# Two-layer hybrid trunk: in the MLP layers the low half of a split weight tile comes from a negated ScalarE copy and an accumulating DMA

## The chip, the cores and the metric

The kernel runs on one core of a Trainium2 chip. The number that counts is the device time in microseconds, the median of three runs: 1920.09 us (1918.94, 1920.09 and 1925.68). The profile is one further execution, whose own time is its span.

## What is computed

A trunk of two layers over 512 latent tokens and 256 context tokens, 1024 features wide. Each layer has a mixer (attention and spatial gating in layer 0, retention in layer 1) and then a gated MLP with a depthwise convolution of width 3 along the tokens. Around each sub-layer stand RMS norms, and a shift, scale and gate computed from a conditioning vector by the matrices `ada_w`. The change touches the MLP alone:

```python
D_MODEL, SEQ, CTX_LEN, DEPTH, D_FF, CONV_W = 1024, 512, 256, 2, 2816, 3

def conv_ffn(h, w_in, conv_w, conv_b, w_out):
    a = dwconv3(h @ w_in, conv_w, conv_b)
    gate, up = jnp.split(a, 2, axis=-1)
    return (jax.nn.silu(gate) * up) @ w_out

# in layer i, for the latent tokens; for the context tokens in layer 0 alone
    h = modulate(rmsnorm(x, norm_g[i, 2]), sh2, sc2)
    x = x + g2 * rmsnorm(conv_ffn(h, ffn_w_in[i], ffn_conv_w[i], ffn_conv_b[i], ffn_w_out[i]), norm_g[i, 3])
```

`w_in` is 1024 x 5632, `w_out` 2816 x 1024, all float32.

## The kernel before

**Split products.** Every large product is made in three passes on TensorE in a rounded 32-bit format (fp32r). An operand is held as two tiles: *hi*, the operand rounded to that format, and *lo*, the operand less hi. `mm3` (L86 to L90) computes hi times hi (L88), hi times lo (L89) and lo times hi (L90). So each pass of a weight needs both tiles. In the tile names the last letter is `r` for the raw tile, `h` for hi and `l` for lo.

**Units.** Weights come in units of 128 x 1024 float32, 524,288 bytes. `unit` (L67 to L72) takes a raw tile from a ring of three buffers (tag `raw`), loads it by a DMA that SyncE (SP) issues (`load`, L49 to L50), and calls `split` (L63 to L65): ScalarE (ACT) makes hi by a rounding copy (L64), VectorE (DVE) makes lo by a subtraction (L65). `slot` (L74 to L78) gives hi and lo their place: six pairs in turn in the MLP of layer 0, eight in that of layer 1 (`phase`, L80 to L84).

**The MLP.** `ffn` (from L1101) walks over 22 blocks j of 128 gate and 128 up features. For each block `project` takes two units, f`l`0`j` and f`l`1`j` (f012 is layer 0, the up half, block 2), and multiplies them with the normed input: `pc` is the product for the context tokens (hc, layer 0 only), `pf` that for the latent ones (hl). The first two blocks are done together (four units: f000, f010, f001, f011 in layer 0), with the latent tokens in two halves, since the input of the second half is still being made then. `gated` (L1148 to L1159) applies the convolution and the gate, and splits the result into g. Every second block, `w_out` takes two units fo`l``j` of the output matrix for two earlier blocks, and `out_pieces` (L376 to L395) adds their products (`wf`) into y on DVE (L391). So a layer has 44 f units and 22 fo units.

**Background jobs.** After every block, `bg(2)` moves on a background job by two steps. A job, `ada_half` (L193 to L255), computes half of a later shift, scale or gate: it clears an accumulator on POOL (L199), loads four raw tiles `ar` **from the same ring of three buffers**, and adds each into the accumulators on DVE: two operations per tile and token stream (L208). During the MLP of layer 0 there are six jobs with two streams (24 raw tiles, four DVE operations each), during that of layer 1 two jobs with one stream (8 raw tiles, two operations each).

**The start of an MLP** overlaps the end of the mixer before it. There `residual` (L298 to L319) and `build_h` (L331 to L355) make the MLP's input: ACT squares and sums (L274), POOL scales the sum (L279: wxb, wyb, wyd ...) and takes its power of -1/2 (L260: yb3r, xd3r ...), DVE and ACT apply it (L309, L318, L319: yr), TensorE transposes, ACT applies the shift and scale (L348: hb, hd) and rounds (L64: hl0b, hl0d).

**Order.** A scheduler puts the instructions of each engine into one fixed order when the program is built; each engine then works through its own order and waits on semaphores. This holds for SP and POOL too, where they issue DMAs. A load into a raw buffer waits until the last reader of that buffer's former content is done.

Of the kernel before, what the change touches and what calls it, by code (L numbers as in the profile page):

```python
# [36 lines left out]
class Trunk:  # L37
# [29 lines left out]
    def unit(self, src, name, dst=None):  # L67
        raw = self.bp.tile([P, 1024], F32, name=f"{name}r", tag="raw", bufs=3)
        self.load(raw, src)
        hi, lo = dst or self.slot(name)  # L70
        self.split(hi, lo, raw)
        return hi, lo  # L72
# [7 lines left out]
    def phase(self, ctx, name, extra):  # L80
        self.xp = ctx.enter_context(self.tc.tile_pool(name=name, bufs=1))
        self.extra = extra
        self.turn = 0
        return self.xp  # L84

# [42 lines left out]
    def ada_first(self, q, pool, native, tag):  # L128
        """shift and scale of a quarter of the features, latent and context, for the first sub-layer; a step per unit"""
        S, V, T = self.S, self.V, self.T  # L130
# [125 lines left out]

# [1 line left out]
    def rsq(self, w, name):  # L258
# [9 lines left out]
    def ssq(self, src, name, n):  # L268
        """mean square over the row, a half (n) at a time"""
        ss = self.sst.get(name)  # L270
        if ss is None:
            ss = self.sst[name] = self.bp.tile([P, 2], F32, name=f"ss{name}", tag="ss", bufs=8)
        junk = self.t2k(f"j{name}{n}", BF16)
        self.S.activation(junk, src, AF.Square, scale=1.0 / 32, accum_out=ss[:, n : n + 1])  # L274
# [23 lines left out]
    def residual(self, t, y, gate, src, last, name, xt):  # L298
        """y (final) -> x += rmsnorm(y) * gate; then x normed into y's place."""
        V = self.V  # L300
        self.load(xt, src)
        hv = [slice(0, 512), slice(512, 1024)]
        for n, h in enumerate(hv):
            self.ssq(y[:, h], f"y{name}{t}", n)
        for h in hv:
            V.tensor_tensor(out=y[:, h], in0=y[:, h], in1=gate[:, h], op=ALU.mult)
        r = self.rms(f"y{name}{t}")
        for n, h in enumerate(hv):
            V.scalar_tensor_tensor(out=xt[:, h], in0=y[:, h], scalar=r, in1=xt[:, h], op0=ALU.mult, op1=ALU.add)  # L309
            if last:  # L310
                self.load(self.out[t * P : (t + 1) * P, h], xt[:, h])
            else:
                self.ssq(xt[:, h], f"x{name}{t}", n)
        if last:
            return
        self.load(self.xd[t], xt)
        r = self.rms(f"x{name}{t}")
        V.tensor_scalar(out=y[:, hv[0]], in0=xt[:, hv[0]], scalar1=r, scalar2=None, op0=ALU.mult)  # L318
        self.S.activation(y[:, hv[1]], xt[:, hv[1]], AF.Copy, scale=r)  # L319
# [11 lines left out]
    def build_h(self, chunk, xn, ab, name):  # L331
        """chunk 2: context tokens, chunks 0 and 1: latent halves."""
        s = 1 if chunk == 2 else 0
# [23 lines left out]
    def hcols(self, t):  # L357
        """stationary views of token tile t: k -> (hi, lo)"""
        if t >= 4:
            c = slice((t - 4) * P, (t - 3) * P)  # L360
            return lambda k: (self.hc[0][:, k, c], self.hc[1][:, k, c])
        c = slice(t * P, (t + 1) * P)
        return lambda k: (self.hl[0][:, k, c], self.hl[1][:, k, c])

    def proj_t(self, ps, w, stream, half=None):
        """ps[feat, tokens] += w^T h, w a stationary unit"""
        h = self.hc if stream else self.hl
# [6 lines left out]

# [1 line left out]
    def out_pieces(self, feats, wo, y, toks, first, final, name, tag="B"):  # L376
        """y[t] (+)= sum over the group's feature tiles, one closure per half token tile;
        feats: list of (hi, lo)[feat, tokens]"""

# [21 lines left out]
    def out_last(self, A, B, y, toks, early, final, name):  # L401
        """the last two groups (feats, wo): group A of the early tokens, group B of these, both for the others"""
        e, o = toks[:early], toks[early:]
# [6 lines left out]
    def finisher(self, gates, src, ab, name, xts, last=False):  # L410
        """per finished token tile: the residual update, then the next sub-layer's input once a chunk is there"""
        done = {}
# [20 lines left out]

# [1 line left out]
    def sgu(self, y, xn):  # L435
# [178 lines left out]
    def project_pair(self, j, pr):  # L614
        """q, k, v of two heads, transposed; returns the steps"""
        w = [self.unit(self.a["hyb_qkv"][(4 * i + j) * P : (4 * i + j + 1) * P], f"w{'qkv'[i]}{j}") for i in range(3)]
# [56 lines left out]
    def bias_tiles(self, h, hd):  # L673
        """8 x (relative bias, or the mask) of the three kinds of query tile"""
        G, ap = self.G, self.ap
# [13 lines left out]
    def score(self, h, b, pr, hd):  # L689
        """softmax of one query tile (b = 4: both context tiles), queries on partitions"""  # L690
        S, V, T, ap = self.S, self.V, self.T, self.ap
# [63 lines left out]
    def weigh(self, h, b, pr, hd):  # L755
        """keys onto partitions, and after a head's last tile the weighted values"""
        S, V, T = self.S, self.V, self.T
# [35 lines left out]

# [1 line left out]
    def retention(self, y, final):  # L795
        S, V, T, G, a = self.S, self.V, self.T, self.G, self.a
        KS = float(np.float32(P) ** np.float32(-0.5))
        with ExitStack() as ctx:
# [19 lines left out]
            def decay(h):  # L818
                """powers of the two decays: within a chunk, of the keys, of the queries, of a chunk"""
                d = hd[h]  # L820
# [35 lines left out]
            def k_nat(h):  # L856
                """keys onto partitions, decayed towards the end and towards the start of their chunk:
                [token tile of the chunk, direction, (context, latent), dk]"""
                d = hd[h]
# [20 lines left out]
            def states(h):  # L880
                """sums of key x value before (forwards) and behind (backwards) each chunk: [chunk, direction, dv]"""
                d = hd[h]
# [216 lines left out]

# [1 line left out]
    def ffn(self, l, y, final):  # L1101
# [192 lines left out]
def stat(w):  # L1294
    """[1024, n] -> tiles [n/128 * 128, 8 * 128]: row p of tile j holds w[k*128+p, j*128+c] as (k, c)"""
    n = w.shape[1]
    return w.reshape(KD, P, n // P, P).transpose(2, 1, 0, 3).reshape(-1, 1024)


def mov(w, width):  # L1300
    """[1024, n] -> units of 1024 / width row blocks by width columns"""
    n, g = w.shape[1], 1024 // width
    return w.reshape(KD // g, g, P, n // width, width).transpose(3, 0, 2, 1, 4).reshape(-1, 1024)


def cols(v):
    """[m, 1024-multiple] -> [128, ...] one column per block of 128"""
    return v.reshape(-1, P).T
# [52 lines left out]
```

## Time and profile before

| What | Value |
|---|---|
| median of three runs | 1920.09 us |
| span of the profiled execution | 1922.2 us |
| mean granted TensorE clock | 0.990 |
| MLP of layer 0, from its first unit's conversion to its last product | about 409 to 986 us |
| MLP of layer 1, from its first products to about its end | about 1532 to 1900 us |
| DMA, mean over the span | 104 GB/s |

How to read the profile: PE is TensorE's matmuls, PEld its weight loads, which overlap them; DVE is VectorE, ACT ScalarE, POOL GpSimd, SP SyncE, SPq the DMAs that SP issues. A row of instructions names its source line, the engine, the operation, the tiles (out<-in) and a count. In rows of a tile, three durations follow in ns (shortest, median, longest) and the starts of the first and the last instruction in us. In rows of the time line stand start and duration in us, and in brackets how long the engine had been idle before and what released it. The line given is often a helper's, so the tile's name tells what a row belongs to.

### The profile page before, as it was taken

What the parts mean: (1) busy time and instruction counts of PE and PEld (TensorE: products, weight loads), DVE (VectorE), ACT (ScalarE), POOL (GpSimd) and SP (SyncE); (2) the same over time, 40 slices, a digit from 0 to 9 for tenths busy, and PEclk for the clock granted to TensorE, in tenths of its full rate; (3) what the DMA queues carried; (4) which work ended last, traced back from release to release, by engine and by line L of the source; (5) the groups of instructions that cost most, each with busy time, mean ns of one, the idle gap of its engine ahead of it and who ended that gap; (6) DMA issues with size and microseconds to landing.
All of it is one profiled execution on the core that took longest, in us unless ns stands there. A gap on an engine that the chain in (4) does not pass through costs nothing. (4 is left out here: it accounts for less than half of the span.)

```text
span 1922.2 us, 26580 instructions
## 1 busy us (share of the span) xinstructions
PE 1856.5 (97%) x10544; PEld 1567.6 (82%) x10544; DVE 1274.3 (66%) x2103; ACT 811.5 (42%) x1340; POOL 166.0 (9%) x249
## 2 busy tenths in 40 slices
PE   7998989989999999999989999999999899999998
PEld 4886867678888888888879889988999787888886
DVE  4844688679698755555577666676655696566565
ACT  6533545665432323222365434443444454333322
POOL 1102222130000000000021110011001100000001
PEclk9999999999999999999999999999999999999999
DMA  7323332143444311122334313331421254332222
GB/s 287 113 97 104 94 103 90 47 143 116 139 143 132 100 65 47 64 66 66 110 114 132 126 53 109 115 105 46 131 67 56 99 185 157 99 99 92 95 66 88
DMA packets 58301, 199.88 MB, mean 104 GB/s; under 512 B 7200, under 2 KB 8736, under 8 KB 58176
## 3 DMA queue, kind: packets, MB, share of 16 engines
q1 hardware_dynamic: 58176, 198.17, 31.5%
q8 instruction: 83, 1.36, 0.3%
q14 instruction: 42, 0.34, 0.1%
HBM read 187.66 MB, written 10.49 MB: 103 GB/s over the span
## 5 line engine op out<-in xcount | busy, mean ns | idle before, releaser
L208 DVE SCALAR_TENSOR_TENSOR acc<-ar,cs,acc 128x512 f32<-128x512 f32 x256 | 189.2, 759 | 21.3 <-DMA ar<-in_adaw 8.9
L391 DVE TENSOR_TENSOR yf<-wf,yf 128x512 f32<-128x512 f32 x160 | 110.0, 689 | 53.0 <-PE wf L90 52.7
L1148 ACT ACTIVATE cv<-pf,cw 128x512 f32<-128x512 f32 x88 | 67.4, 766 | 38.3 <-PE pf L90 38.2
L64 ACT ACTIVATE g<-cv 128x768 fp32r<-128x768 f32 (+1 forms) x44 | 32.6, 740 | 120.0 <-DVE cv L1157 120.0
L1149 DVE SCALAR_TENSOR_TENSOR cv<-pf,cw,cv 128x511 f32<-128x511 f32 x88 | 65.6, 745 | 16.9 <-ACT cv L1148 16.8
L1152 DVE SCALAR_TENSOR_TENSOR cv<-pf,cw,cv 128x511 f32<-128x511 f32 x88 | 65.8, 747 | 1.7
L1156 ACT ACTIVATE cv<-cv 128x768 f32<-128x768 f32 (+1 forms) x44 | 32.3, 734 | 39.4 <-DVE cv L1152 39.4
L199 POOL MEMSET acc<- 128x512 f32 x32 | 16.8, 527 | 336.8 <-DVE al L65 236.1
L1148 ACT ACTIVATE cv<-pc,cw 128x256 f32<-128x256 f32 x44 | 24.8, 564 | 49.4 <-PE pc L90 25.6
L65 DVE TENSOR_TENSOR g<-cv,g 128x768 fp32r<-128x768 f32 (+1 forms) x44 | 36.2, 822 | 12.6 <-ACT g L64 11.8
L1157 DVE TENSOR_TENSOR cv<-cv,cv 128x768 f32<-128x768 f32 (+1 forms) x44 | 36.1, 821 | 0.5
L960 DVE SCALAR_TENSOR_TENSOR of<-rx,e,of 128x256 f32<-128x256 f32 x64 | 28.9, 478 | 8.4 <-PE rx L90 7.9
L980 POOL TENSOR_SCALAR rrr<-rmv 128x2 f32<-128x2 f32 x16 | 3.1, 193 | 363.1 <-DVE rmv L977 363.1
L751 ACT ACTIVATE sc<-sc,sst 128x512 f32<-128x512 f32 x32 | 23.1, 721 | 23.1 <-DVE sc L742 22.6
L279 POOL TENSOR_SCALAR wye<-ssye 128x1 f32<-128x1 f32 x4 | 2.7, 673 | 348.3 <-ACT jye L274 348.3
L391 DVE TENSOR_TENSOR yr<-wr,yr 128x512 f32<-128x512 f32 x40 | 27.5, 688 | 5.2 <-PE wr L90 4.8
L279 POOL TENSOR_SCALAR wyc<-ssyc 128x1 f32<-128x1 f32 x6 | 4.2, 699 | 291.5 <-ACT jyc L274 291.5
L870 ACT ACTIVATE kd<-kn,e 128x256 fp32r<-128x256 f32 x32 | 14.0, 475 | 35.7 <-PE kn L867 31.5
L65 DVE TENSOR_TENSOR rv<-rn,rv 128x512 fp32r<-128x512 f32 x24 | 16.5, 686 | 18.1 <-ACT rv L64 18.1
L1149 DVE SCALAR_TENSOR_TENSOR cv<-pc,cw,cv 128x255 f32<-128x255 f32 x44 | 21.1, 479 | 9.8 <-ACT cv L1148 9.8
L986 DVE TENSOR_SCALAR on<-of,rmv,rrr 128x256 f32<-128x256 f32 x32 | 18.1, 603 | 11.8 <-POOL rrr L983 11.8
L695 PE MATMUL s<-ka,q 128*128 128x256 f32 x80 | 24.0, 321 | 1.3 <-ACT sc L708 1.1
(2836 smaller groups left out, 6928.2 us busy)
## 6 DMA issues: line engine op xcount, KB each, us to landing
ar<-in_adaw SPq DMA_DIRECT2D x96, 512.0 KB
xd<-xd SPq DMA_DIRECT2D x8, 512.0 KB
xn<-in_x SPq DMA_DIRECT2D x6, 512.0 KB
ngr<-in_norm_g SPq DMA_DIRECT2D x12, 256.0 KB
xb<-in_x SPq DMA_DIRECT2D x6, 512.0 KB
xd<-xb SPq DMA_DIRECT2D x6, 512.0 KB
xc<-xd SPq DMA_DIRECT2D x6, 512.0 KB
xd<-xc SPq DMA_DIRECT2D x6, 512.0 KB
```

The costliest lines, as they stand in the source:

```text
L64: self.S.activation(hi, src, AF.Copy)
L65: self.V.tensor_tensor(out=lo, in0=src, in1=hi.bitcast(F32), op=ALU.subtract)
L208: V.scalar_tensor_tensor(out=acc[s], in0=raw[:, kk * 512 : kk * 512 + 512], scalar=self.cs[:, 8 * s + k : 8 * s + k + 1], in1=acc[s], op0= ...
L391: self.V.tensor_tensor(out=y[t][:, o], in0=ps, in1=y[t][:, o], op=ALU.add)
L695: T.matmul(out, q[:, cols], keys(ka), start=True, stop=False)
L751: S.activation(sc, sc, AF.Exp, bias=st[:, 0:1], scale=-1.0, accum_out=st[:, 1:2])
L960: V.scalar_tensor_tensor(out=d["o"][:, t], in0=ps[:, n], scalar=d["e"][n][:, 386 + i : 387 + i], in1=d["o"][:, t], op0=ALU.mult, op1=ALU.add,)
L1148: S.activation(d, s, AF.Identity, scale=w1, bias=b)
L1149: V.scalar_tensor_tensor(out=d[:, 1:n], in0=s[:, 0 : n - 1], scalar=w0, in1=d[:, 1:n], op0=ALU.mult, op1=ALU.add)
L1152: V.scalar_tensor_tensor(out=d[:, 0 : n - 1], in0=s[:, 1:n], scalar=w2, in1=d[:, 0 : n - 1], op0=ALU.mult, op1=ALU.add)
L1156: S.activation(act[0], act[0], AF.Silu)
L1157: V.tensor_tensor(out=act[0], in0=act[0], in1=act[1], op=ALU.mult)
```

## The change

In `unit`, in the two MLP phases (whose names begin with "ffnp"), the call of `split` is replaced. ACT makes hi as before, and then a second copy of the raw tile with scale -1.0 into the lo tile, whose format rounds it the same way, so that lo holds -hi. Then POOL issues a DMA from the raw tile into lo that adds to what is there: raw - hi. All other uses of `split` stay, those of g and of the ada accumulators among them.

```diff
         raw = self.bp.tile([P, 1024], F32, name=f"{name}r", tag="raw", bufs=3)
         self.load(raw, src)
         hi, lo = dst or self.slot(name)
-        self.split(hi, lo, raw)
+        if self.stage:
+            self.S.activation(hi, raw, AF.Copy)
+            self.S.activation(lo, raw, AF.Copy, scale=-1.0)
+            self.G.dma_start(lo, raw, accum_op=ALU.add)
+        else:
+            self.split(hi, lo, raw)
         return hi, lo
...
         self.extra = extra
         self.turn = 0
+        self.stage = name.startswith("ffnp")
         return self.xp
```

The rest of the diff takes out doc strings and comments. 132 units are concerned, 66 in each layer. In the fixed order of each engine nothing moves outside the two MLP phases and the overlap at their starts. ACT runs the second copy right behind the first or a few instructions later. On POOL the DMAs stand in line with its other work: at the start of layer 0's MLP f000's stands behind xb1r, f010's before wyb3, f001's behind yb3r; in layer 1 f100's and f110's stand behind yd2r and yd3r, f101's behind xd3r. A raw buffer's next load waits for the accumulating DMA in place of the subtraction: f011's for that of f000, and in the regular part of layer 1 each load for that of the unit three before. In layer 0 one buffer serves f012, f003, f013 and fo00 one after another, and later f005, f015, fo02 and fo03, while ada raw tiles lie in the others.

## The prediction

> **What bounds the kernel now.** First the page: the span and the engines' busy time.
>
> ```profile
> span 1922.2 us, 26580 instructions
> PE 1856.5 (97%) x10544; PEld 1567.6 (82%) x10544; DVE 1274.3 (66%) x2103; ACT 811.5 (42%) x1340; POOL 166.0 (9%) x249
> ```
>
> PE sets the end: all other time in the span is 1922.2 − 1856.5 = 65.7 us. DVE, which the change relieves, has a third of the span free. So the change can gain only where PE stands still in the two MLP phases, and lose only where it makes PE stand still there. The view of busy time by stretches shows how much that is (columns after the length: busy us of PE, PEld, DVE, ACT, POOL with counts, granted clock, DMA share, GB/s).
>
> ```profile
> 408.00:455.00 47.00, 41.80 (x332) 39.38 (x331) 41.93 (x67) 30.56 (x57) 6.97 (x10) 1.00 0.45 149
> 455.00:500.00 45.00, 45.00 (x243) 38.25 (x242) 39.29 (x55) 22.54 (x32) 1.58 (x3) 1.00 0.42 141
> 500.00:960.00 460.00, 459.82 (x2420) 387.07 (x2418) 299.60 (x424) 142.31 (x185) 5.24 (x10) 1.00 0.28 89
> 1530.00:1566.00 36.00, 32.37 (x230) 30.35 (x230) 31.11 (x47) 23.40 (x42) 5.51 (x7) 0.89 0.51 173
> 1566.00:1600.00 34.00, 33.68 (x145) 26.51 (x145) 30.11 (x39) 21.03 (x30) 0.00 (x0) 1.00 0.68 213
> 1600.00:1896.00 296.00, 296.00 (x1277) 238.85 (x1278) 178.37 (x227) 100.28 (x124) 0.00 (x0) 1.00 0.28 91
> ```
>
> Layer 0's MLP is the first three rows, layer 1's the others. In the long rows PE never waits. Its idle time is at the starts: 5.2 us in the first row, 3.6 and 0.3 us in the fourth and fifth, 9.1 us in all. There DVE is nearly full (41.93 of 47, 31.11 of 36).
>
> How far ahead of PE are the weights? The tile view gives a unit's conversion and its first matmul (min/median/max ns, then first and last start).
>
> ```profile
> L88 PE MATMUL pf<-hl0d,f1012h x8: 390/392/398, 1726.5 to 1739.6; 128*128 128x512 f32 x8
> L64 ACT ACTIVATE f1012h<-f1012r x1: 1066/1066/1066, 1701.8 to 1701.8; 128x1024 fp32r<-128x1024 f32 x1
> L65 DVE TENSOR_TENSOR f1012l<-f1012r,f1012h x1: 1215/1215/1215, 1703.1 to 1703.1; 128x1024 fp32r<-128x1024 f32 x1
> ```
>
> f1012 is one of the shortest leads in the long stretches: from 1701.8 to 1726.5, less 2.3 for the two operations, it lies finished 22.4 us before use. At a phase's start there is no such lead, and the chain of waits shows what paces the weights:
>
> ```profile
> 1581.81 4.42 DMA f104r<-in_ffn_in
> 1586.24 1.08 ACT f104h L64
> 1587.35 1.24 DVE f104l L65
> 1588.60 3.32 DMA f105r<-in_ffn_in
> ```
>
> A raw buffer is one of three. Load, rounded copy, subtract, and only then the next load into it: that is a serial link, here near 5.9 us, and it is what the change lengthens.
>
> **What the change costs, part by part.** It takes 132 subtractions off DVE (44 + 22 units, two layers: 132 × 1.22 = 161 us), adds 132 ACT copies (132 × 1.06 = 140 us) and 132 accumulating DMAs of 0.52 MB that POOL issues. Both engines' totals stay far below PE's, so these sums cost or gain nothing by themselves: ACT rises from 42% to about 50%. What counts is the link, since a raw buffer now comes free only when the accumulating DMA has read it.
>
> No row shows an accumulating DMA, or any DMA that POOL issues. Call X the time from the end of the second ACT copy until it has landed. Below: it moves as much as a load, so 3.3 us, the shortest load above. Above: 4.42 us, the longest load above, plus two more passes of the data (the destination must be read as well, and written while both are read), plus a queueing time on POOL.
>
> ```profile
> q1 hardware_dynamic: 58176, 198.17, 31.5%
> 1540.24 2.62 POOL L279 TENSOR_SCALAR wyd<-ssyd 128x1 f32<-128x1 f32 x1 [5.49 <-ACT jyd L274]
> ```
>
> A pass is 1.6 us: 31.5% of 1922.2 us is 605 us for 198.17 MB, so 0.524 MB take 1.6 us of all 16 engines. The longest POOL row near a start is 2.62 us. Upper bound 4.42 + 3.2 + 2.62 = 10.2 us. I take 6.5: an ordinary load, 3.5, one more pass, 1.6, and 1.4 for POOL's turn, about half its longest row. It is nearer to the load's end because the data and its size are a load's.
>
> The Trainium skill ("DMA: Bandwidth & Descriptors", the section Anatomy of one DMA) gives for GpSimd-issued DMAs a fixed part near 2 us plus the bytes at about 436 GB/s. By that X would be an estimated 3.2 us and the time that of the first rival below; it says nothing there of accumulating, and no row of this trace can confirm it.
>
> A link is then 3.5 (load) + 2 × 1.06 (ACT) + 6.5 = 12.1 us. Before it was:
>
> ```profile
> 504.11 0.33 SPq L50 DMA_DIRECT2D f015r<-in_ffn_in  x1
> 509.99 0.33 SPq L50 DMA_DIRECT2D fo02r<-in_ffn_out  x1
> ```
>
> 5.9 us from issue to issue. Where all three buffers turn, the ring gives one unit in 12.1/3 = 4.0 us. PE spends 8.3 us on a unit in layer 0 (f002 to f012 below, 454.8 to 463.1) and 5.6 us in layer 1 (eight steps of 0.70). So the long stretches hold: extra latency 2 × 1.06 + 6.5 − 2.3 = 6.3 us against a lead of 22.4 us. Nothing is lost there up to X = 11.2, where (5.6 + X)/3 passes 5.6.
>
> The starts are different. In the changed program's static order, units and ada raws share the ring, SP issues in order, and long runs of units follow one another through one buffer while ada raws sit in the others.
>
> *Layer 0.*
>
> ```profile
> 419.63 0.62 ACT L64 ACTIVATE hl0b<-hb 128x512 fp32r<-128x512 f32 x1
> 423.90 0.62 ACT L274 ACTIVATE jyb<-ysg 128x512 bf16<-128x512 f32 x1
> 426.59 0.56 POOL L260 TENSOR_TENSOR yb3r<-wyb,mhalf 128x1 f32<-128x1 f32 x1
> L88 PE MATMUL pc<-hc0b,f002h x8: 276/276/276, 454.8 to 457.2; 128*128 128x256 f32 x8
> L88 PE MATMUL pc<-hc0b,f012h x8: 276/276/281, 463.1 to 465.5; 128*128 128x256 f32 x8
> L64 ACT ACTIVATE f012h<-f012r x1: 1058/1058/1058, 444.7 to 444.7; 128x1024 fp32r<-128x1024 f32 x1
> L65 DVE TENSOR_TENSOR f012l<-f012r,f012h x1: 1217/1217/1217, 457.3 to 457.3; 128x1024 fp32r<-128x1024 f32 x1
> L208 DVE SCALAR_TENSOR_TENSOR acc<-ar,cs,acc 128x512 f32<-128x512 f32 x256 | 189.2, 759 | 21.3 <-DMA ar<-in_adaw 8.9
> L88 PE MATMUL wf<-fo03h,g x12: 392/397/401, 541.4 to 558.4; 128*128 128x512 f32 x12
> ```
>
> f001's two copies come on ACT behind the second jyb (424.5), and its DMA stands on POOL behind yb3r, which ends at 427.2: it lands at 433.7. Behind it on SP comes an ada raw (437.2), then DVE works on two raws, each 4 × 0.759 = 3.0 us and an estimated 1.5 us of other DVE work: 446.2. Then f012 loads and lands at 446.2 + 12.1 = 458.3. Through the same buffer follow f003, f013, fo00: 3 × 12.1 = 36.3, at 494.6. Now two ada raws (load 3.5, DVE 9.0): 507.1; f004 and f014 together (3.5 + 4 × 1.06 + 6.5): 521.3; f005, f015, fo02, fo03: 4 × 12.1 = 48.4, at 569.7. PE used fo03 at 541.4. Smaller stops before lie inside that: f010's DMA waits behind hl0b (420.25 + 1.05 + 6.5), and f011 lands only at about 440, so that f002 begins 7 us late. PE loses 569.7 − 541.4 = **28.3 us**. The sum holds X ten times.
>
> *Layer 1.*
>
> ```profile
> 1546.93 0.73 ACT L319 ACTIVATE yr<-xd,xd3r 128x512 f32<-128x512 f32 x1 [1.16 <-POOL xd3r L260]
> L88 PE MATMUL pf<-hl0d,f104h x8: 390/392/404, 1592.9 to 1605.6; 128*128 128x512 f32 x8
> ```
>
> POOL's xd3r precedes yr, so f101's DMA starts before 1548; f111's copies follow yr after an estimated 2.2 us (f101's added copy and its own wait), end at 1552 and its DMA lands at 1558.5. An ada raw's load 3.5, DVE 2.5 on it (two operations of 0.759 and 1 us estimated beside them) and SP's 0.4: f112 issues at 1564.9 and lands at 1577.0; f103, fo11, f104 follow by 12.1 each: 1613.3. Before, f104's main run began at about 1605.6 − 7 × 0.70 = 1600.7. PE loses **12.6 us**, with X five times.
>
> Sum: 1922.2 + 28.3 + 12.6 = 1963.1 us of span. The profiled span lies 2.1 us above the median 1920.09, so 1961 us. One us of X is worth 15 us. X = 3.3 leaves only the late f011 and f111 (4.3 + 3.0 = 7.3 us: 1927); X = 10.2 adds 3.7 × 15 = 55: 2016.
>
> **The rivals.**
>
> *A, a cheap accumulate.* X at or below 4: the chains stay within the leads and the time is about 1927, within what counts as the same. For it: DMA engines are 28 to 68% busy in these stretches and bytes grow by a third only. Against it: it needs no slower handling of read-add-write than of a plain copy, and POOL prompt.
>
> *B, faster.* f012's copy ended at 445.8, but DVE reached its subtraction at 457.3: 11.5 us of queueing. With DVE's 1.22 us a unit gone, ada raws release their buffers sooner. If X plus the second copy stays clearly below that queueing, X under about 3 us, and the ada raws' DVE work loses its 1.5 us of waiting, the starts could close. It gives at most the 9.1 us of PE's idle time there: 1911 us. Against it: f011 and f111 had next to no queueing and are on the path.
>
> *C, a slow accumulate.* X beyond 11.2: the ring then bounds the long stretches too. At X = 12 the starts cost 40.9 + 5.5 × 15 = 123 us; layer 1's ring gives a unit in 17.6/3 = 5.87 us against 5.6, 0.27 × 52 units = 14 us, and about as much in layer 0, where 24 ada raws pass the same buffers: 151 us, 2071 us. For it: three streams of data per DMA in place of two, on engines that reach 213 GB/s at a start. Against: the bound of 10.2.
>
> The Trainium skill ("SBUF — State Buffer", the section Who interferes with whom) warns that GpSimd's descriptor writing can be held up by some of VectorE's fast modes. That would be a way to C; no row here shows it.
>
> **How the numbers follow.** Forecast (X from 4 to 10.2) 0.63; A 0.13; B 0.05; C 0.16; 0.03 for a release I misread. About 0.5%, 9.6 us, is what a measurement of this kernel can tell from no change. Faster 0.04 (most of B), same 0.13 (A, less its upper edge), slower 0.83. The range runs from A's 1926 to 2030, a little beyond X = 10.2, with some 2 in 10 outside, mostly C.
>
> **What would show it.** The accumulating DMAs' issue-to-landing time in the list of DMAs says which X holds. PE's idle time should lie at 455 to 570 and 1566 to 1614, and stay near nothing between there and each phase's end. Waits of the matmuls on fo02/fo03 and f104 should end with a DMA into the low tile. Stops evenly through the long stretches would make C right; a DVE chain still setting the starts would make me wrong altogether.

## The result, and the profile after

The changed kernel takes 2005.91 us (median of four runs, 2001.30 to 2009.84) against 1919.51 for the kernel before: a ratio of 1.0439 (95% interval 1.0413 to 1.0465), 86 us slower. The direction and the range of the prediction held; its 41 us was less than half of the loss.

The page of the changed kernel, the lines that answer to those of before, and the new queue:

```profile
span 1999.4 us, 26850 instructions
PE 1872.6 (94%) x10544; PEld 1577.8 (79%) x10544; DVE 1131.9 (57%) x1971; ACT 931.6 (47%) x1472; POOL 277.2 (14%) x381
q1 hardware_dynamic: 58176, 198.17, 30.5%
q0 software_dynamic: 19008, 69.21, 18.9%
```

The profiled span is 77.2 us longer. PE stands still for 1999.4 − 1872.6 = 126.8 us in place of 65.7, that is 61.1 more, and is busy 16.1 us longer with the same 10,544 matmuls. DVE's row falls by 142.4 us (1274.3 to 1131.9; less than the 161 us of the subtractions' durations, since a row counts the overlap of neighbouring instructions once), and that brings nothing.

Busy time by stretches, with columns as before (PE's first, then after the engines the granted clock, the DMA share and GB/s):

```profile
408.00:455.00 47.00, 33.19 (x213) 31.30 (x212) 27.24 (x46) 24.38 (x45) 10.70 (x16) 0.82 0.65 182
500.00:600.00 100.00, 90.23 (x436) 73.87 (x435) 51.86 (x80) 44.07 (x57) 12.38 (x16) 0.95 0.65 168
600.00:700.00 100.00, 87.85 (x439) 72.86 (x439) 61.96 (x98) 40.84 (x52) 11.60 (x16) 0.93 0.67 169
800.00:900.00 100.00, 100.00 (x530) 84.91 (x529) 42.96 (x65) 39.96 (x49) 10.32 (x12) 1.00 0.55 126
...
1630.00:1650.00 20.00, 15.36 (x56) 11.90 (x55) 7.38 (x11) 9.85 (x12) 2.57 (x3) 0.83 0.97 221
1670.00:1690.00 20.00, 18.00 (x78) 14.21 (x76) 4.98 (x7) 11.27 (x13) 3.44 (x4) 1.00 0.98 221
1690.00:1710.00 20.00, 8.21 (x28) 6.59 (x29) 7.99 (x12) 9.51 (x12) 3.44 (x4) 0.66 0.98 216
1740.00:1800.00 60.00, 60.00 (x259) 48.31 (x259) 23.91 (x34) 31.57 (x37) 9.45 (x11) 1.00 0.83 191
```

Late in both phases PE is full, as forecast. But the stops in layer 0 go on to about 705 us, not to 570, and layer 1 has its worst one at 1690, where no stop was forecast. Where the stops lie the granted clock is down, to 0.66 in the worst stretch, and matmuls right behind a stop take longer (shown in the last section): the 16 us of added busy time go with that.

What PE waited for, by the view of waits, first in layer 0's MLP, then in layer 1's (total, times, longest):

```profile
PE at L247 <- DVE acc L214: 9.1, 1, 9.1
PE wf L94 <- DVE yf L397: 7.1, 3, 3.6
PE htb L348 <- DVE hb L356: 5.9, 1, 5.9
PE wf L94 <- ACT yf L395: 4.1, 1, 4.1
PE pc L96 <- DMA f011l<-f011r: 3.5, 1, 3.5
PE wf L95 <- DMA fo01l<-fo01r: 2.6, 1, 2.6
```

```profile
PE wf L94 <- DVE yf L397: 13.8, 1, 13.8
PE pf L96 <- DMA f103l<-f103r: 4.6, 1, 4.6
PE pf L94 <- ACT f101h L72: 3.5, 1, 3.5
```

Waits that end with an accumulating DMA come to some 17 us in all (with smaller ones not shown). The larger part, 43.5 us in the other rows shown, ends with an instruction of DVE or ACT, and most of these handle no weight: an addition into y (yf), an ada accumulation (acc), the input's shift and scale (hb). Why were those late? The time line of ACT ahead of the worst stop (the bracket gives the idle time before an instruction and what ended it):

```profile
1670.24 1.06 ACT L72 ACTIVATE fo12h<-fo12r 128x1024 fp32r<-128x1024 f32 x1 [2.16 <-DMA fo12r<-in_ffn_out]
...
1679.76 1.06 ACT L72 ACTIVATE f106h<-f106r 128x1024 fp32r<-128x1024 f32 x1 [2.26 <-DMA f106r<-in_ffn_in]
1680.72 1.04 ACT L73 ACTIVATE f106l<-f106r 128x1024 fp32r<-128x1024 f32 x1
...
1694.80 1.06 ACT L72 ACTIVATE f117h<-f117r 128x1024 fp32r<-128x1024 f32 x1 [2.99 <-DMA f117r<-in_ffn_in]
...
1698.63 1.06 ACT L72 ACTIVATE fo14h<-fo14r 128x1024 fp32r<-128x1024 f32 x1 [1.31 <-DMA fo14r<-in_ffn_out]
1699.59 0.76 ACT L1154 ACTIVATE cv<-pf,cw 128x512 f32<-128x512 f32 x1
```

The same moments on DVE, on PE, and PE's use of f106:

```profile
1700.39 0.75 DVE L1155 SCALAR_TENSOR_TENSOR cv<-pf,cw,cv 128x511 f32<-128x511 f32 x1 [7.02 <-ACT cv L1154]
1701.05 0.68 DVE L397 TENSOR_TENSOR yf<-wf,yf 128x512 f32<-128x512 f32 x1
```

```profile
1701.79 0.80 PE L94 MATMUL wf<-fo12h,g 128*128 128x512 f32 x1 [13.79 <-DVE yf L397]
```

```profile
L94 PE MATMUL pf<-hl0d,f106h x8: 394/394/394, 1712.0 to 1716.9; 128*128 128x512 f32 x8
```

ACT works through its fixed order: the copies of fo12, f106 and so on up to fo14, each standing 1.3 to 3.0 us before a raw tile that has not come. Behind fo14's first copy comes a conv activation (cv, L1154), behind that DVE's cv, behind that the addition into y, and PE cannot go on before that addition has emptied a product bank. PE stands 13.79 us although f106, copied at 1679.76, is not used until 1712.0. At this stop the weights were in time for PE; they were late for ACT.

### The profile page after: what moved, and what is told of

Read it like the earlier page. It is cut to its first block, busy times and chain, and to the rows that moved or that the text cites. A ratio compares the mean times of both kernels' runs of the same rounds, so it can differ in the third digit from the quotient of the medians.

```text
span 1999.4 us, 26850 instructions
## 1 busy us (share of the span) xinstructions
PE 1872.6 (94%) x10544; PEld 1577.8 (79%) x10544; DVE 1131.9 (57%) x1971; ACT 931.6 (47%) x1472; POOL 277.2 (14%) x381
## 3 DMA queue, kind: packets, MB, share of 16 engines
q1 hardware_dynamic: 58176, 198.17, 30.5%
q0 software_dynamic: 19008, 69.21, 18.9%
## 5 line engine op out<-in xcount | busy, mean ns | idle before, releaser
L1154 ACT ACTIVATE cv<-pf,cw 128x512 f32<-128x512 f32 x88 | 67.1, 763 | 29.2 <-PE pf L96 29.1
L1158 DVE SCALAR_TENSOR_TENSOR cv<-pf,cw,cv 128x511 f32<-128x511 f32 x88 | 65.7, 747 | 2.1
L65 DVE TENSOR_TENSOR g<-cv,g 128x768 fp32r<-128x768 f32 (+1 forms) x44 | 36.3, 824 | 29.2 <-ACT g L64 29.2
L1154 ACT ACTIVATE cv<-pc,cw 128x256 f32<-128x256 f32 x44 | 24.7, 562 | 35.6 <-DVE cv L1158 29.2
L757 ACT ACTIVATE sc<-sc,sst 128x512 f32<-128x512 f32 x32 | 23.0, 719 | 23.0 <-DVE sc L748 22.5
L65 DVE TENSOR_TENSOR rv<-rn,rv 128x512 fp32r<-128x512 f32 x24 | 16.5, 686 | 18.1 <-ACT rv L64 18.1
L691 POOL TENSOR_TENSOR tm<-slab,mask 128x256 f32<-128x256 f32 x16 | 16.9, 1076 | 62.2 <-DVE sst L738 62.0
L64 ACT ACTIVATE rv<-rn 128x512 fp32r<-128x512 f32 x24 | 14.2, 593 | 24.0 <-PE rn L96 24.0
L64 ACT ACTIVATE ah<-acc 128x512 fp32r<-128x512 f32 x32 | 19.6, 626 | 12.3 <-DVE acc L214 12.1
L65 DVE TENSOR_TENSOR al<-acc,ah 128x512 fp32r<-128x512 f32 x32 | 22.2, 697 | 5.3 <-PE ag L231 3.5
```

The source lines that it names most:

```text
L64: self.S.activation(hi, src, AF.Copy)
L65: self.V.tensor_tensor(out=lo, in0=src, in1=hi.bitcast(F32), op=ALU.subtract)
L1154: S.activation(d, s, AF.Identity, scale=w1, bias=b)
L1158: V.scalar_tensor_tensor(out=d[:, 0 : n - 1], in0=s[:, 1:n], scalar=w2, in1=d[:, 0 : n - 1], op0=ALU.mult, op1=ALU.add)
```

## The experiments

Fifteen further kernels ran. "Ratio" is against the kernel before, run on the same chip.

| Run | Median, us | Ratio, 95% interval |
|---|---|---|
| changed kernel | 2005.91 | 1.0439 (1.0413 to 1.0465) |
| hold: DMA sums into a scratch tile, DVE makes lo | 2032.35 | 1.0568 (1.0547 to 1.0589) |
| early: only the 50 units of the starts | 2001.72 | 1.0420 (1.0400 to 1.0439) |
| slots: layer 1 with five slots | 1993.49 | 1.0368 (1.0349 to 1.0388) |
| startsplit: first four units by DVE | 1991.27 | 1.0356 (1.0335 to 1.0377) |
| traffic: before, and 132 DMAs more | 1979.56 | 1.0302 (1.0273 to 1.0332) |
| hbm: sum taken from HBM | 1976.24 | 1.0274 (1.0257 to 1.0291) |
| adaxp3: ada raws in a ring of their own | 1972.23 | 1.0257 (1.0242 to 1.0273) |
| ring6: six raw buffers | 1971.11 | 1.0258 (1.0243 to 1.0273) |
| plain: copy in place of sum | 1960.35 | one run |
| ring6start: ring6 and startsplit | 1953.87 | 1.0167 (1.0151 to 1.0183) |
| ring6plain: ring6 and plain | 1953.83 | 1.0167 (1.0152 to 1.0182) |
| late: only the other 82 units | 1931.08 | 1.0048 (1.0031 to 1.0065) |
| dveadd: ACT copy, DVE addition | 1926.37 | 1.0024 (1.0013 to 1.0034) |
| badaxp3: before, with adaxp3's rings | 1921.10 | 0.9991 (0.9981 to 1.0000) |
| bring6: before, with six raw buffers | 1919.92 | 0.9990 (0.9980 to 0.9999) |

How late PE is at some units, in us: the start of its first matmul with the unit in that run's profile, less the same in the kernel before (f002 454.8, fo03 541.4, fo09 696.4, f101 1546.9, f114 1606.3, fo15 1657.5, fo121 1896.9). The last column is the mean time from one load's issue to the next in the start of layer 1, from f102r to fo15r, over 17 steps; some ada loads lie between.

| Run | f002 | fo03 | fo09 | f101 | f114 | fo15 | fo121 | load pace |
|---|---|---|---|---|---|---|---|---|
| before | 0 | 0 | 0 | 0 | 0 | 0 | 0 | 3.1 |
| changed | 14.1 | 25.9 | 51.0 | 46.1 | 61.5 | 77.6 | 77.2 | 5.2 |
| hbm | 11.4 | 20.8 | 31.7 | 30.2 | 54.1 | 54.1 | 53.7 | 4.3 |
| adaxp3 | 15.3 | 24.9 | 24.5 | 20.9 | 48.5 | 48.5 | 48.2 | 5.6 |
| slots | 11.7 | 27.1 | 55.2 | 51.7 | 70.1 | 72.5 | 72.4 | 5.5 |
| startsplit | −0.1 | 11.3 | 42.6 | 40.4 | 50.2 | 64.3 | 63.9 | 5.4 |
| plain | 2.5 | 6.5 | 20.8 | 16.5 | 26.8 | 36.7 | 36.3 | 4.7 |
| ring6 | 15.2 | 24.6 | 26.6 | 22.5 | 47.4 | 47.4 | 47.0 | 4.6 |
| ring6plain | 8.1 | 10.5 | 10.0 | 10.4 | 26.9 | 27.0 | 26.6 | 3.9 |
| late | −0.5 | −0.7 | 5.3 | 6.4 | 6.7 | 6.7 | 6.3 | 3.1 |

### Is it the low tiles, the ring, or the second copy?

**hold.** The low tile is DVE's again; the DMA sums into a scratch tile.

```diff
-            self.S.activation(hi, raw, AF.Copy)
-            self.S.activation(lo, raw, AF.Copy, scale=-1.0)
-            self.G.dma_start(lo, raw, accum_op=ALU.add)
+            self.split(hi, lo, raw)
+            scr = self.xp.tile([P, 1024], F32R, name=f"{name}s", tag="scr", bufs=2)
+            self.S.activation(scr, raw, AF.Copy, scale=-1.0)
+            self.G.dma_start(scr, raw, accum_op=ALU.add)
```

> The low tile is made by DVE's subtraction as before; the negated copy and the accumulating DMA are made too, but into a scratch tile that nobody reads, so that the raw buffer is held as long as in the changed kernel while PE never waits for a DMA's sum. ACT and POOL do what they do in the changed kernel, DVE what it did before. Ring theory: nearly all of the loss stays, 1980 to 2015 us. Late-low-tile theory: 1920 to 1940. DMA or POOL load theory: as the ring theory; the run with the sum taken from HBM tells these two apart.

It took 2032.35 us, above even the ring theory's span. No matmul waits for a sum here, yet the loss is larger than in the changed kernel. Part of that may be the run's own: DVE keeps its subtractions, and ACT waits 15 times, 22.9 us in all, for one of only two scratch tiles. The view of PE's waits, layer 0 and then layer 1, largest rows:

```profile
PE wf L95 <- DVE yf L398: 17.1, 13, 4.0
PE at L248 <- ACT arow L245: 8.0, 3, 3.6
```

```profile
PE wf L95 <- DVE yf L398: 20.9, 4, 13.8
PE pf L95 <- ACT f102h L64: 5.2, 1, 5.2
```

It is the same picture without the low tiles: additions into y that come late. A loss of this size needs no low tile that is late for PE; in the changed kernel, by the waits above, such tiles are some 17 of 61 us.

**dveadd.** ACT's two copies as in the changed kernel, and DVE adds.

```diff
-            self.G.dma_start(lo, raw, accum_op=ALU.add)
+            self.V.tensor_tensor(out=lo, in0=lo.bitcast(F32), in1=raw, op=ALU.add)
```

> ACT makes both copies as in the changed kernel, but DVE adds the raw tile to the negated copy; no accumulating DMA. This keeps the 140 us of ACT copies alone. Ring theory: the link is 3.5 + 2.1 + 1.2 us and DVE's queue, about 1 us longer than before, 1920 to 1932 us. A theory by which the second ACT copy is the cost (ACT full at the starts): 1960 or more.

1926.37 us: the 140 us of ACT copies cost some 5 us of the 86. The rest comes with the DMA in place of an addition by DVE.

**hbm.** The sum is taken from HBM, and the raw buffer comes free after the second copy.

```diff
-            self.G.dma_start(lo, raw, accum_op=ALU.add)
+            self.G.dma_start(lo, src, accum_op=ALU.add)
```

> The accumulating DMA adds the tile straight from HBM, not from the raw buffer, so that the raw buffer comes free when ACT's second copy ends (link about 3.5 + 2.1 + gaps, near the 5.9 us of before, against some 12 of the changed kernel). Low tiles come as late as in the changed kernel, POOL issues the same 132 DMAs and HBM is read 69 MB more. Ring theory (a raw buffer held about 6 us longer makes later loads late, and ACT and DVE, which work in order, stand before late tiles with work behind them that PE needs): most of the 86 us comes back, 1930 to 1950 us, and PE's stops behind DVE acc and DVE yf in the middle of the phases are gone. Late-low-tile theory (PE waits for the accumulated tiles themselves): as the changed kernel, 1990 to 2010. DMA or POOL load theory: as the changed kernel or above, 2000 to 2040.

1976.24 us: about a third of the loss comes back, not most of it. The ring theory alone was too simple. Such a sum took longer, from the end of the second copy to landing 7.7 us in the median of layer 0 against 5.0. Loads came later as well: at the start of layer 1, where ACT waited for one, its copy began 7.2 us after the load's issue (median of 8), against 5.5 in the changed kernel (of 14) and 3.5 before (of 8).

**adaxp3.** In the MLP phases ada raws turn through three buffers of their own.

```diff
-            raw = self.bp.tile([P, 1024], F32, name=f"ar{l}{half}{kp}", tag="raw", bufs=3)
+            raw = (self.xp if self.stage else self.bp).tile(
+                [P, 1024], F32, name=f"ar{l}{half}{kp}", tag="rawa" if self.stage else "raw", bufs=3
+            )
```

> The changed kernel, but in the two MLP phases the ada raw tiles have a ring of three buffers of their own, so the units turn through three buffers alone. With links near 12 us a unit can come every 4 us, against 8.3 and 5.6 us of PE per unit. Ring theory: the stops in the middle go, the late first units stay (about 14 us in layer 0 and some 6 in layer 1): 1935 to 1955 us. DMA or POOL load theory: 1990 to 2015. Late-low-tile theory: 1990 to 2010.

1972.23 us, between the theories. The table of lateness shows where: after fo03 layer 0 loses nothing more (24.9, then 24.5, against 25.9 and 51.0), so layer 0's later stops go with the shared ring, where late ada tiles held DVE and PE. (Three more buffers for the units do the same there: ring6 below, 24.6 and 26.6.) In layer 1, which has only eight ada raws, one long stop stays, in the view of PE's waits:

```profile
PE wf L94 <- ACT yf L397: 14.2, 1, 14.2
```

### Is it ACT's run through the free slots?

**slots.** Layer 1 with five slots.

```diff
-            fp = self.phase(ctx, f"ffnp{l}", 3 if l == 0 else 5)
+            fp = self.phase(ctx, f"ffnp{l}", 3 if l == 0 else 2)
```

> The changed kernel with five slots for split units in layer 1's MLP in place of eight. In the changed kernel ACT's fixed order has the copies of f104 to fo14 ahead of the conv activations that DVE's y additions, and through them PE, wait for; each copy waits about 5 us for its late raw tile, and PE stands 13.8 us at fo12 although f106 to f117 lie ready more than 20 us before their use. Run-ahead theory (ACT fills the free slots in one go at the ring's pace, and PE waits behind it): with five slots there is less to fill, PE's loss between f111 and fo14 falls from 29 us to 18 or less, and the time to 1990 to 1998 us. Lead theory (a shorter lead is what exposes late units): the loss grows, 2010 us or more.

1993.49 us. Fewer slots make the kernel *faster*, as the run-ahead theory said. PE's lateness grows from f111 (54.9) to fo14 (72.5) by 17.6 us, in place of 29.5 in the changed kernel (48.1 to 77.6), and the longest wait for yf in layer 1 is gone from the top of the list:

```profile
PE pf L96 <- DMA f103l<-f103r: 4.4, 1, 4.4
PE wf L95 <- DMA fo11l<-fo11r: 2.6, 1, 2.6
...
PE wf L94 <- DVE yf L397: 1.8, 2, 1.5
```

**startsplit.** The first four units of each MLP by DVE.

```diff
-        if self.stage:
+        if self.stage and name not in FIRST:
...
+FIRST = ("f000", "f010", "f001", "f011", "f100", "f110", "f101", "f111")
```

> The changed kernel, but the first four units of each MLP (f000, f010, f001, f011 and f100, f110, f101, f111) are split by DVE as before. In the changed kernel's trace PE is 14 us late at f002 and another 6 at f102. If those late first units are a cost of their own: 1983 to 1992 us. If the late start only gives the later units time, and the ring makes up for it with longer stops behind: within 6 us of the changed kernel, 2000 to 2010.

1991.27 us, within the first of the two spans: the late first units are a cost of their own, some 15 us (with six buffers, ring6 less ring6start, 17 us).

**late** and **early.** The 50 units of the starts by DVE and the rest by DMA, and the reverse.

```diff
-        if self.stage:
+        if self.stage and not self.first(name):
...
+    def first(self, name):
+        k = (10, 8) if name[1] != "o" else (8, 6)
+        return int(name[3:]) < k[int(name[2 if name[1] == "o" else 1])]
```

> The changed kernel, but the units at the start of each MLP (layer 0: f of blocks 0 to 9 and fo 0 to 7; layer 1: f of blocks 0 to 7 and fo 0 to 5; 50 of 132) are split by DVE as before; 82 units keep the negated copy and the accumulating DMA. Theory that the loss lies wholly in the starts, where free slots are filled in one go at the pace of ring and DMA engines: 1918 to 1926 us. If accumulating DMAs cost PE time in the long stretches too: some 82/132 of the loss, 1960 to 1975 us.

> The complement: those 50 units by the negated copy and the accumulating DMA, the other 82 by DVE as before. Starts theory: the whole loss, 1995 to 2012 us. If the loss is spread over the units: 1945 to 1960 us.

late 1931.08 us, early 2001.72: 10 and 80 us above the kernel before, which add up to the whole within the runs' spread. So the loss lies in the starts. In the long stretches of late, with 55% and 82% of the DMA engines busy, PE is full:

```profile
720.00:960.00 240.00, 240.00 (x1271) 203.18 (x1270) 103.37 (x155) 96.05 (x117) 23.55 (x27) 1.00 0.55 133
1700.00:1880.00 180.00, 180.00 (x779) 145.72 (x778) 76.30 (x110) 90.18 (x105) 28.26 (x33) 1.00 0.82 185
```

The 10 us of late are above what was expected. In its profile PE stops once in the long part of layer 0, for 4.0 us at 658.6, where the run goes over from one way to the other, and is 5.3 us late at fo09; up to f114 in layer 1 it loses about 1 us more (6.7).

### Buffers or DMA engines?

**ring6** and **ring6start.** Three raw buffers more, used by every second unit.

```diff
-        raw = self.bp.tile([P, 1024], F32, name=f"{name}r", tag="raw", bufs=3)
+        self.nu += 1
+        if self.stage and self.nu > 4 and self.nu % 2:
+            raw = self.xp.tile([P, 1024], F32, name=f"{name}r", tag="rawx", bufs=3)
+        else:
+            raw = self.bp.tile([P, 1024], F32, name=f"{name}r", tag="raw", bufs=3)
```

> The changed kernel, but from the fifth unit of an MLP on every second unit takes its raw buffer from three further ones, so six turn in all (the ada raws stay with the old three); slots and instructions stay. Links stay long, but a unit can come every 14/6 = 2.3 us in place of 4.7. Ring theory: the stops in the middle of the phases go, the late first units stay (14 us in layer 0, about 6 to 10 in layer 1): 1937 to 1955 us. Contention theory (the DMA engines, not the number of buffers, set when tiles arrive): the same traffic in less time, 1975 us or more.

> As the run with six buffers, and the first four units of each MLP are split by DVE as before. Ring theory with late first units as the only other cost: 1920 to 1935 us. Contention theory: 1960 us or more.

1971.11 and 1953.87 us: both between the two theories. Three more buffers give back 35 us, but a load was still issued only every 4.6 us at the start of layer 1. The stretches of ring6 there show why:

```profile
1600.00:1620.00 20.00, 18.36 (x85) 14.72 (x84) 11.47 (x17) 11.14 (x15) 2.56 (x3) 1.00 0.95 271
1620.00:1640.00 20.00, 11.18 (x44) 8.43 (x43) 8.65 (x13) 13.60 (x18) 4.30 (x5) 0.88 0.99 247
```

The DMA engines are 95 and 99% busy: with the buffers out of the way, they limit the pace here. (In stretches beside these the view gives 1.04 and 1.05; read it as full.)

**plain** and **ring6plain.** A copy in place of the sum; the low half is then the raw tile, and the result another.

```diff
-            self.G.dma_start(lo, raw, accum_op=ALU.add)
+            self.G.dma_start(lo, raw)
```

> The changed kernel with the POOL-issued DMA copying the raw tile into the low tile in place of adding (so the low half is the raw tile, and the result is another). It prices the adding: if a plain copy takes as long as the accumulating DMA, from the end of the second ACT copy to landing about 5.0 us in layer 0 and 6.0 in layer 1 (medians of the changed kernel), the adding itself is free and the time is about 2000 us; if the read-add-write costs a pass more, the copy takes 1 to 1.6 us less and the time falls by some 10 to 25 us.

> Six raw buffers and plain copies in place of accumulating ones (the low half is then the raw tile, another result). By the DMA list the 69 MB of POOL-issued DMAs took 18.9% of 16 engines over 1999 us when accumulating, 2.9 us a unit, and 10.0% over 1959 us as plain copies, 1.5 us; a load takes 1.6. If with six buffers the DMA engines set the pace at the starts (4.5 us a unit), 3.1 us a unit must take most of the rest of the middle loss away: 1938 to 1952 us (PE starts late by some 5 us in layer 0 and 4 in layer 1, as with three buffers and plain copies). If something else than DMA engines and buffers sets it (ACT's two copies, POOL): 1955 to 1965 us, little below the plain copies with three buffers.

plain took 1960.35 us, 46 less than the changed kernel, above the 10 to 25 that were expected. The lists of DMAs, first of the changed kernel, then of plain with its queue's row (last column of a DMA: us from issue to landing, here at a lightly loaded moment):

```profile
f003l<-f003r POOLq DMA_DIRECT2D x1, 512.0 KB, 4.5
```

```profile
q0 software_dynamic: 19008, 69.21, 10.0%
...
f003l<-f003r POOLq DMA_DIRECT2D x1, 512.0 KB, 2.9
```

The adding costs 1.6 us of latency, and the engines 18.9% of 1999.4 us = 378 us for 132 units, 2.9 us each, in place of 10.0% of 1958.6 = 196 us, 1.5 us each. With its load (30.5% of 1999.4 us for 198.17 MB, 1.6 us a unit) a unit of the changed kernel costs all 16 engines 4.5 us; before it cost 1.6. ring6plain came to 1953.83 us, just above the span for "the engines set the pace" and below the other. Its start of layer 1 has these stretches:

```profile
1560.00:1580.00 20.00, 17.54 (x123) 17.30 (x123) 11.66 (x19) 11.88 (x17) 1.59 (x3) 0.83 0.98 320
1580.00:1600.00 20.00, 20.00 (x113) 17.21 (x112) 13.25 (x20) 14.37 (x19) 2.77 (x6) 1.00 0.96 342
```

The engines are full there too, at 320 to 342 GB/s against 247 to 293 with sums (ring6 from 1580 to 1640), and loads come every 3.9 us in place of 4.6. But its longest stop of layer 1 comes just behind, where they are not full:

```profile
1600.00:1620.00 20.00, 13.75 (x55) 10.78 (x54) 9.36 (x14) 13.36 (x18) 2.52 (x5) 0.87 0.86 294
```

PE stands 6.3 us there before fo10, until ACT's instruction for y: the fixed order again. Some 33 us of the 86 stay with both remedies, and full engines do not explain all of them.

**traffic** was to show contention alone: the kernel before with 132 POOL-issued copies from HBM into a scratch tile.

```diff
             self.split(hi, lo, raw)
+            scr = self.xp.tile([P, 1024], F32, name=f"{name}s", tag="scr", bufs=3)
+            self.G.dma_start(scr, src)
```

> The kernel before, whose units are split on ACT and DVE as ever, with 132 POOL-issued DMAs more, each a plain copy of the unit from HBM into a scratch tile that nobody reads: the traffic and POOL's issues without the ring's longer links. DMA or POOL load theory: most of the 86 us appears, 1975 us or more. Ring theory: 1922 to 1935 us, since loads get slower by contention only a little. The run with the sum taken from HBM kept 54 us of the loss, so a mixed outcome, 1935 to 1965, would give contention a share of its own.

It took 1979.56 us, within the span of the load theory, but does not decide: nothing tied these copies to their units, and POOL sent them ahead as fast as the scratch tiles came free, so that the start of layer 0 is denser than in the changed kernel. Here the same stretch of the changed kernel, then of traffic:

```profile
455.00:500.00 45.00, 44.72 (x303) 40.59 (x303) 29.83 (x47) 24.79 (x34) 4.46 (x6) 1.00 0.52 129
```

```profile
455.00:500.00 45.00, 42.82 (x245) 37.02 (x243) 31.62 (x45) 15.54 (x21) 12.14 (x23) 0.96 0.90 331
```

What it does show is that more traffic, with units split as before and a raw buffer's link no longer by a sum, gives stops of the same kind, here in layer 0:

```profile
PE wf L94 <- ACT yf L395: 12.6, 2, 6.3
PE ag L231 <- DVE cv L1158: 10.7, 2, 8.5
```

**badaxp3** and **bring6** give the kernel before the other rings: the edits of adaxp3 and of ring6 on it.

> The kernel before, with three raw buffers of their own for the ada raws in the MLP phases, no other change. If the ring of three limits the starts of the kernel before as well, part of its 9 us of PE idle time there goes: 1912 to 1919 us. If not, 1918 to 1924.

> The kernel before with the same six raw buffers, split by DVE throughout. Own ada buffers gave it nothing that could be measured, so 1916 to 1923 us; below 1912 would say that its ring of three limits it after all.

1921.10 and 1919.92 us: about a thousandth, and at most two by the intervals. The ring of three does not limit the kernel before, and none of the versions with accumulating DMAs comes down to it.

## Why the prediction was right in part, and where it failed

*What held.* PE bounds the kernel, DVE's relief is worth nothing, a raw buffer's longer link is the harm, and it falls on the starts of the phases. The chain written out for layer 0 was close: fo03's sum was forecast to land at 569.7 us and landed at 568.3 (issue 563.6 and 4.7), PE's loss at fo03 was to be 28.3 us and is 25.9. In layer 1, 12.6 was forecast, at f104; from f101 to f114, the unit behind f104, 61.5 − 46.1 = 15.4 came. But the closeness is partly luck. f012's sum landed at 465.7, 7.4 us later than forecast, and the links behind it were shorter than the 12.1 forecast (10.4 to 12.0 from landing to landing). And PE waited only 0.6 us for fo03's low tile, not at all for f104's: it had lost its time in stops before, in layer 0 more of it behind DVE and ACT than behind sums, in layer 1 most in a wait for f103's sum (4.6 us).

*X* was taken as 6.5 us. Its medians are 5.0 us in layer 0 and 6.0 in layer 1 (4.7 at least, 8.7 at most): within the bounds, lower than taken. Its part for POOL's turn, 1.4 us, was 0.3 in the median and 2.3 at most. By the forecast's slope of 15 us per us that would have made the loss smaller, so X is not the error. (plain shortened the sums by 1.7 and 2.1 us in the medians and gained 46 us, more than that slope gives; but it also halves the engines' time for them, so that it does not measure the slope alone.) The Trainium skill ("DMA: Bandwidth & Descriptors", Anatomy of one DMA) gave an estimated 3.2 us for such a transfer. That agrees with the plain copy (2.9 to 3.0 us when little else runs) and not with the accumulating one (4.5).

*The step that failed* is "So the long stretches hold: extra latency 2 × 1.06 + 6.5 − 2.3 = 6.3 us against a lead of 22.4 us. Nothing is lost there". It took the lead of a unit before its matmul as the time that the unit may be late. But ACT and DVE are between, and keep a fixed order in which the copies of units far ahead stand in front of the conv activations and the additions that PE needs next. A unit that comes late for ACT can stop PE long before its own matmul, whatever its lead. The chains were therefore cut off too early, at fo03 and f104, where the low tiles have caught up with PE: from fo03 to fo09 layer 0 loses a further 25.1 us, from f114 to fo15 layer 1 a further 16.1. Together they are 41 us, and they are what is missing between 40.9 us and 77.2 (some 5 us come back between the layers). PE's stops accordingly did not end at 570 and 1614, as forecast, but at 705 and 1702. For layer 1, slots shows it directly: with fewer slots, and so a shorter lead, the loss is smaller. For layer 0 it is adaxp3 and ring6, in which nothing much is lost behind fo03.

Nor was f1012's 22.4 us the lead to go by. In the kernel before, f006 is used in the same long row, some 2.5 us after its subtraction ends:

```profile
L90 PE MATMUL pc<-hc0b,f006l x8: 276/278/281, 543.7 to 560.1; 128*128 128x256 f32 x8
L65 DVE TENSOR_TENSOR f006l<-f006r,f006h x1: 1217/1217/1217, 539.9 to 539.9; 128x1024 fp32r<-128x1024 f32 x1
```

By the forecast's own rule 6.3 us of extra latency had to cost some 4 us there, and PE's lateness grows from 25.9 at fo03 to 30.3 at f006 (543.5 before, 573.8 after), 1.9 us of it in a wait for f006's sum.

*What was not weighed* is the DMA engines' time. "DMA engines are 28 to 68% busy and bytes grow by a third only" counts bytes; a summed byte takes the engines twice as long, and a unit in the changed kernel 4.5 us where it took 1.6. At the start of layer 1 the kernel before asks for a load every 3.1 us. Neither three buffers (a link there, from a load's issue to that of the unit three later, is 14.2 us in the mean of the six from f115r to fo15r, so 4.7 a unit, not 12.1 and 4.0) nor the engines allow that. The term of the link that was too small there is the load: 3.5 us was taken, and ACT's copy began 5.5 us after the issue in the median, where it waited for one. How much belongs to buffers and to engines isn't settled: buffers alone give back 35 us, cheaper DMAs alone 46, both together 52.

*The start* of layer 0 was taken as 7 us late at f002 and is 14.1. The time line of DVE shows one reason:

```profile
436.55 0.75 DVE L214 SCALAR_TENSOR_TENSOR acc<-ar,cs,acc 128x512 f32<-128x512 f32 x1 [8.10 <-DMA ar<-in_adaw]
437.21 0.48 DVE L324 TENSOR_SCALAR ysg<-xb,xb3r 128x512 f32<-128x512 f32 x1
```

An ada raw came late, and the last token tile's norm (L324) stood behind its accumulation: again the fixed order.

*Rivals.* A and B fell with X. C's mechanism, the ring bounding the long stretches, did not appear: PE is full there at up to 83% of the DMA engines. That GpSimd's descriptor writing be held up by VectorE, of which the Trainium skill warns ("SBUF — State Buffer", Who interferes with whom), isn't seen in the changed kernel: POOL's DMA instructions in the start of layer 0, with DVE 58% busy, took 0.86 to 1.08 us and later 0.85; no run tests it by itself.

## What to carry to other kernels

A tile's lead before its consumer is not the time that it may be late: ask which engine touches it first, what stands behind that in the engine's fixed order, and when PE needs *that*. When a step is moved to a DMA, count the engines' time per unit and set it against the fastest pace that any stretch of the kernel asks for, not against the mean. And more buffers for finished tiles can hurt, if a slow producer then fills them all before other work gets its turn.

## What the runs showed of the hardware

A POOL-issued accumulating DMA of 512 KB within SBUF took 4.5 us from issue to landing when little else ran, a plain one 2.9; of the 16 engines' time it took 2.9 us against 1.5. In stretches where such sums and loads filled the engines to 95% and more, they moved 203 to 293 GB/s by the profile's count of bytes, with plain copies in place of the sums 320 to 342. And stops cost more than their length: 61 us of added idle time came with 16 us of slower matmuls. At the 13.8 us stop the granted clock was 0.51 in the mean from 1692.0, 4 us after PE's last matmul, to 1705.6, 4 us after its next:

```profile
1692.00:1705.60 13.60, 3.81 (x9) 3.04 (x10) 5.23 (x8) 7.62 (x9) 2.14 (x4) 0.51 0.95 203
```

The first matmul behind the stop took 0.80 us and the next eight 0.62 to 0.63, where 0.39 is usual.
